# Attention scores of two heads together, in three passes over 64 rows each, in a one-core transformer block

## The chip, the cores and the metric

The kernel runs on one core of a Trainium2 chip. Its time is the device time of that core in microseconds, from three executions; a profiled execution of its own gives the trace. TensorE is called PE, its weight loads PEld, VectorE DVE, ScalarE ACT, GpSimd POOL and SyncE SP.

## The reference, cut to what matters

One residual block on a sequence of 1024 with model width 1024, in float32: a norm, one projection to the operands of eight stick-breaking heads and four differential heads of width 64 (each differential head has two score maps) and to two gates, the two attentions, output projections that are gated and added, a second projection, and a squared-ReLU MLP.

```python
z = jnp.einsum('bhqd,bhkd->bhqk', qb, kh).astype(jnp.float32) * scale      # stick-breaking
w = jnp.where(causal, jnp.exp(log_beta + tail), 0.0)
...
s = jnp.einsum('bhqd,bhkd->bhqk', qb, kh).astype(jnp.float32) * scale + bias   # differential
a = probs(q1b, k1h) - lam * probs(q2b, k2h)
```

A score sums over a head width of 64. TensorE is 128 rows high, and a matmul sums over its rows.

## The kernel before, in words

Matmuls run in a float32 form that rounds its operands, so the kernel splits each operand into a high part (the rounded value) and a low part (the rest) and adds products of parts. A projection takes three: high by high, high by low, low by high.

The attention is done in eight units, four of stick-breaking heads and four of differential ones; a unit holds two heads, or the two maps of one differential head. `project` computes 128 columns of the projection, which are the two heads' q (or k) one below the other: rows 0 to 63 and rows 64 to 127. `project_q` makes of this, for each head, one tile of 128 rows: the head's high part in its own 64 rows and its low part in the other 64. `project_k` makes, for each head, a tile with the high part and a tile with the low part, and copies each by DMA into the other 64 rows too. So a score needs two passes over all 128 rows: (q high over q low) with k high in both halves, and the same q with k low in both halves. `scores` issues these two matmuls (L262, L263) into one of two PSUM banks with the tag `sc`.

`steps_sb` goes through the two heads of a unit one after the other, each with the pairs of query tiles in the order 3, 1, 2, 0. For a query tile of 128 rows the keys up to the diagonal are taken in chunks of up to 512 columns. ScalarE empties a score bank with two sigmoids (L322, L323), GpSimd masks the diagonal block (L326), VectorE scans and multiplies (L331, L332). `steps_diff` does both maps of a query tile: VectorE adds the bias and keeps a running minimum (L389), ScalarE takes the exponential (L394). Score tiles come from pools: `big_s` of 1024 columns for query tiles 4 to 7 and `small_s` of 512 for the others, four buffers each.

When a pair of query tiles is done, `finish_sb` or `finish_diff` transposes the weights on PE (L281), splits them and multiplies them with v (L300, L301, or L342 to L344). These calls stand one step late, behind the next scores. Between the steps the main loop inserts filler: the projections of the next unit (L196 to L198, L243 to L245) and of the gates, dealt out in proportion to the steps' weights. What the program writes is then put in order by a scheduler, engine by engine, so matmuls written one after the other can end up with others between them; PE works strictly in that final order. A small matmul over 32 rows (L433, three times) builds the bias table between the first scores.

After the attention the outputs come back from DRAM as tiles `y` and go through the gated projections, the second projection and the MLP, which the change does not touch beyond the pools that `y` and the gates use.

Of the kernel before, what the change touches and what calls it, by code (L numbers as in the profile page):

```python
# [16 lines left out]
P = 128  # L17
# [24 lines left out]
def hybrid_block_kernel(  # L42
# [38 lines left out]
    def f32(ap):  # L81
        return ap.bitcast(F32)
# [67 lines left out]
    with ExitStack() as actx:  # L150
# [4 lines left out]
        def normalised(c):  # L155

            xs = []
            for t in range(4 * c, 4 * c + 4):
                if t == 6:
                    last = pa.tile([P, 2, D], F32, tag="v", name="x_67", bufs=3)  # L160
                if t < 6:
                    xt = pa.tile([P, D], F32, tag="big_s" if t < 4 else "kh", name=f"x_{t}", bufs=4)
                else:
                    xt = last[:, t - 6, :]
# [39 lines left out]
        def project_q(blk, name, scale, qs):  # L204

            qs += [pa.tile([P, S], F32R, tag="qs", name=f"qs_{name}_{a}", bufs=4) for a in range(2)]

            def done(c, cs, acc):
                for a, (own, other) in enumerate(((LO, HI), (HI, LO))):
                    nc.scalar.activation(qs[a][own, cs], acc[own], AF.Copy, scale=scale)  # L210
                    nc.vector.scalar_tensor_tensor(
                        qs[a][other, cs], acc[own], scale, f32(qs[a][own, cs]),
                        op0=ALU.mult, op1=ALU.subtract,
                    )

            yield from project(blk, name, done)

        def project_k(blk, name, kh, kl):

            kh += [pa.tile([P, S], F32R, tag="kh", name=f"kh_{name}_{a}", bufs=4) for a in range(2)]  # L220
            kl += [pa.tile([P, S], F32R, tag="kl", name=f"kl_{name}_{a}", bufs=4) for a in range(2)]

            def done(c, cs, acc):
                for a, own in enumerate((LO, HI)):
                    nc.scalar.copy(kh[a][own, cs], acc[own])
# [33 lines left out]
        def scores(qs, kh, kl, qt, c0, c1, name):  # L259
            z = ps.tile([P, HALF], F32, tag="sc", name=name, bufs=2)  # L260
            q = qs[:, qt * P:(qt + 1) * P]
            nc.tensor.matmul(z[:, :c1 - c0], q, kh[:, c0:c1], start=True, stop=False)  # L262
            nc.tensor.matmul(z[:, :c1 - c0], q, kl[:, c0:c1], start=False, stop=True)  # L263
# [48 lines left out]
        def steps_sb(u, qs, kh, kl, v):  # L312
            for a in range(2):
                for j in ORDER:
                    w = []
                    for qt in (2 * j, 2 * j + 1):
                        nk = (qt + 1) * P
                        name = f"{u}_{a}_{qt}"
                        beta, rest = score_tile(qt, f"beta_{name}"), score_tile(qt, f"rest_{name}")
                        for c0, c1 in chunks(nk):  # L320
                            z = scores(qs[a], kh[a], kl[a], qt, c0, c1, f"z_{name}_{c0}")
                            nc.scalar.activation(rest[:, c0:c1], z, AF.Sigmoid, scale=-1.0)  # L322
                            last_sigmoid[0] = nc.scalar.activation(beta[:, c0:c1], z, AF.Sigmoid)  # L323
                        dg = slice(nk - P, nk)
# [10 lines left out]
                        w.append(beta)  # L335
# [749 lines left out]
```

## Time and profile before

| | |
|---|---|
| median of 3 runs | 1466.37 us (1465.51 to 1468.13) |
| profiled execution | 1466.14 us, span 1464.4 us |
| granted TensorE clock | 0.999 |
| busy share of the span | PE 98%, PEld 83%, DVE 70%, ACT 51%, POOL 22% |
| matmuls | 7302 records |

A busy PE is not a PE at its peak, since matmuls overlap and their ends are modelled: the time from the start of one to the start of the next is what it occupies. In a timeline row the columns are the start, the length, the engine, the line, the operation, output and inputs, height and width of the weights, output shape and count, and in brackets the idle time before and what ended it. In a row of a group of instructions, the numbers behind the bar are busy time, mean length of one in ns, and idle time before them with what ended it.

### The profile page before, as it was taken

The numbers are of one execution on the slowest core, as the hardware profiler recorded it, in microseconds if no ns is written. First come the engines' busy times: TensorE is split into PE (matmuls) and PEld (weight loads), VectorE is DVE, ScalarE is ACT, GpSimd is POOL, SyncE is SP. The second block draws the span as 40 slices with busy tenths as digits, with TensorE's granted clock in tenths as the row PEclk, the third lists the DMA queues.
The fourth block names the chain that finished last, engine by engine and source line by source line (L and its number), as shares of the span: only waits on it lengthen the run. The fifth ranks groups of instructions, "written<-read, shape, count | busy, mean of one in ns | idle before, by whom it ended". The sixth has DMA issues, their size and how long they took to land. (4 is left out here: it accounts for less than half of the span.)

```text
span 1464.4 us, 20068 instructions
## 1 busy us (share of the span) xinstructions
PE 1437.3 (98%) x7302; PEld 1219.3 (83%) x7302; DVE 1021.1 (70%) x1468; ACT 743.2 (51%) x1352; POOL 322.4 (22%) x312
## 2 busy tenths in 40 slices
PE   7999999999999999999999989999999999999997
PEld 6888898899889888888888868788888778888886
DVE  5487987898779866535555489767664589764783
ACT  6356766676556645753434464444444344534450
POOL 2022231231000000000002326333330357232611
PEclk9999999999999999999999999999999999999999
DMA  5342212221322244554357735544445676677681
GB/s 205 77 133 66 69 48 80 68 70 51 91 72 67 85 136 173 178 181 146 131 159 233 244 115 195 182 158 147 139 155 200 216 274 190 200 239 273 203 287 58
DMA packets 93402, 219.45 MB, mean 150 GB/s; under 512 B 9228, under 2 KB 24824, under 8 KB 93304
## 3 DMA queue, kind: packets, MB, share of 16 engines
q1 hardware_dynamic: 78904, 198.25, 42.5%
q10 hardware_dynamic: 14400, 19.93, 3.7%
q8 instruction: 57, 0.93, 0.3%
q14 instruction: 41, 0.34, 0.1%
HBM read 152.07 MB, written 60.05 MB: 145 GB/s over the span
## 5 line engine op out<-in xcount | busy, mean ns | idle before, releaser
L331 DVE TENSOR_TENSOR_SCAN rest<-rest 128x896 f32<-128x896 f32 (+3 forms) x64 | 87.7, 1375 | 20.5 <-POOL rest L326 19.9
L198 PE MATMUL acc_gate<-h_hi,lo_gate 128*128 128x512 f32 x256 | 101.0, 394 | 0.0
L196 PE MATMUL acc_gate<-h_hi,hi_gate 128*128 128x512 f32 x256 | 100.8, 394 | 0.0
L197 PE MATMUL acc_gate<-h_lo,hi_gate 128*128 128x512 f32 x256 | 100.7, 393 | 0.0
L608 DVE TENSOR_TENSOR lS_lo<-raw_S,lS_hi 128x1024 fp32r<-128x1024 f32 x32 | 58.6, 1831 | 39.9 <-ACT lS_hi L607 39.8
L326 POOL TENSOR_SCALAR_AFFINE_SELECT rest<-rest 128x128 f32<-128x128 f32 x64 | 24.3, 379 | 239.7 <-ACT rest L322 223.2
L955 PE MATMUL dS<-rT_hi,lS_hi 128*128 128x512 f32 x192 | 74.7, 389 | 0.0
L955 PE MATMUL dS<-rT_lo,lS_hi 128*128 128x512 f32 x192 | 74.7, 389 | 0.0
L955 PE MATMUL dS<-rT_hi,lS_lo 128*128 128x512 f32 x192 | 74.7, 389 | 0.0
L607 ACT CAST lS_hi<-raw_S 128x1024 fp32r<-128x1024 f32 x32 | 33.7, 1052 | 78.2 <-DMA raw_S<-s_dramS 46.6
L567 PE MATMUL mix<-y,hi_mix 128*128 128x512 f32 x256 | 68.6, 389 | 0.0
L394 ACT ACTIVATE s<-s,low 128x896 f32<-128x896 f32 (+7 forms) x64 | 49.7, 776 | 28.0 <-DVE low L389 27.8
L389 DVE CUSTOM_DVE_ANT_0 s<-z,bias 128x512 f32<-128x512 f32 (+3 forms) x64 | 37.0, 587 | 31.7 <-PE z L263 26.7
L567 PEld LDWEIGHTS mix<-y,hi_mix 128*128 128x128 f32 x256 | 48.1, 188 | 9.9
L198 PEld LDWEIGHTS acc_gate<-h_hi,lo_gate 128*128 128x128 f32 x256 | 48.2, 188 | 9.2
L197 PEld LDWEIGHTS acc_gate<-h_lo,hi_gate 128*128 128x128 f32 x256 | 48.2, 188 | 8.8
L116 POOL TENSOR_SCALAR rstd_o<-s 128x1 f32<-128x1 f32 x8 | 3.0, 380 | 237.8 <-DMA grow<-in_g_rows_dram 213.0
L196 PEld LDWEIGHTS acc_gate<-h_hi,hi_gate 128*128 128x128 f32 x256 | 48.2, 188 | 8.6
L608 DVE TENSOR_TENSOR lA_lo<-raw_A,lA_hi 128x1024 fp32r<-128x1024 f32 x24 | 37.5, 1561 | 24.9 <-ACT lA_hi L607 23.3
L287 ACT CAST wth_sb<-tr_sb 128x512 fp32r<-128x512 f32 (+1 forms) x80 | 41.2, 548 | 26.5 <-PE tr_sb L281 25.1
L326 POOL TENSOR_SCALAR_AFFINE_SELECT beta<-beta 128x128 f32<-128x128 f32 x64 | 53.7, 838 | 3.2 <-ACT beta L323 2.1
L288 DVE TENSOR_TENSOR wtl_sb<-tr_sb,wth_sb 128x512 fp32r<-128x512 f32 (+1 forms) x80 | 48.5, 627 | 7.7 <-ACT wth_sb L287 7.5
(350 smaller groups left out, 4766.3 us busy)
## 6 DMA issues: line engine op xcount, KB each, us to landing
s_dramS<-us SPq DMA_DIRECT2D x64, 256.0 KB, 3.7
raw_S<-s_dramS SPq DMA_DIRECT2D x32, 512.0 KB, 4.6
s_dramA<-u ACTq DMA_DIRECT2D x48, 256.0 KB, 2.3
raw_A<-s_dramA SPq DMA_DIRECT2D x24, 512.0 KB, 3.9
raw_gate<-in_w_in_dram SPq DMA_DIRECT2D x16, 512.0 KB, 3.6
gate_dram<-gt SPq DMA_DIRECT2D x32, 256.0 KB, 2.4
y<-y_dram SPq DMA_DIRECT2D x16, 512.0 KB, 6.0
g<-gate_dram SPq DMA_DIRECT2D x16, 512.0 KB, 4.4
```

What stands on the lines that cost most here:

```text
L196: nc.tensor.matmul(acc, w_hi[:, ks], h_hi[k][:, cs], start=(k == 0), stop=False)
L197: nc.tensor.matmul(acc, w_hi[:, ks], h_lo[k][:, cs], start=False, stop=False)
L198: nc.tensor.matmul(acc, w_lo[:, ks], h_hi[k][:, cs], start=False, stop=(k == NK - 1))
L287: nc.scalar.copy(hi[:, :n], tr[:, :n])
L288: nc.vector.tensor_tensor(lo[:, :n], tr[:, :n], f32(hi[:, :n]), op=ALU.subtract)
L326: nc.gpsimd.affine_select(tl[:, dg], tl[:, dg], pattern=[[-1, P]], compare_op=ALU.is_gt, fill=fill, base=0, channel_multiplier=1,)
L331: nc.vector.tensor_tensor_scan(back, back, back, 1.0, op0=ALU.mult, op1=ALU.bypass)
L389: nc.vector.tensor_tensor_reduce(out=s[:, c0:c1], in0=z, in1=bias[:, S - nk + c0:S - nk + c1], scale=1.0, scalar=BIG if prev is None else ...
L394: e = nc.scalar.activation(s[:, :nk], s[:, :nk], AF.Exp, bias=low, scale=-1.0, accum_out=sums[:, m:m + 1],)
L567: nc.tensor.matmul(accs[i][c], st[:, ks], mv[:, cs], start=(first and k % 4 == 0), stop=(last and k % 4 == 3),)
L608: nc.vector.tensor_tensor(lo, raw, f32(hi), op=ALU.subtract)
L955: nc.tensor.matmul(acc, st[:, e, ts], mv[:, e, :], start=(first and e == 0 and i == 0), stop=(last and e == 1 and i == 2))
```

## The change

q and k are kept as projected: one tile of 128 rows with the high parts of both heads and one with the low parts, made by one function for both. The copies into the other half go. A score is now three passes over the 64 rows of its head (high q by high k, low q by high k, high q by low k), and the passes of the two heads are written alternately, rows 0 to 63 for the one and 64 to 127 for the other, each into its own `sc` bank. Both heads of a query tile are therefore worked on together, and their `finish` calls come together. Score tiles have six buffers of each kind; the tiles for `y`, the first x tiles and the first v weights move to other tags.

```diff
-        def project_q(blk, name, scale, qs):
-
-            qs += [pa.tile([P, S], F32R, tag="qs", name=f"qs_{name}_{a}", bufs=4) for a in range(2)]
+        def project_split(blk, name, tag, scale, parts):
+
+            parts += [pa.tile([P, S], F32R, tag=tag, name=f"{tag}_{name}_{p}", bufs=4) for p in range(2)]
+            hi, lo = parts
 
             def done(c, cs, acc):
-                for a, (own, other) in enumerate(((LO, HI), (HI, LO))):
-                    nc.scalar.activation(qs[a][own, cs], acc[own], AF.Copy, scale=scale)
-                    nc.vector.scalar_tensor_tensor(
-                        qs[a][other, cs], acc[own], scale, f32(qs[a][own, cs]),
-                        op0=ALU.mult, op1=ALU.subtract,
-                    )
+                nc.scalar.activation(hi[:, cs], acc, AF.Copy, scale=scale)
+                nc.vector.scalar_tensor_tensor(
+                    lo[:, cs], acc, scale, f32(hi[:, cs]), op0=ALU.mult, op1=ALU.subtract,
+                )
 
             yield from project(blk, name, done)
-
-        def project_k(blk, name, kh, kl):
...
-                for a, own in enumerate((LO, HI)):
-                    nc.scalar.copy(kh[a][own, cs], acc[own])
-                    nc.vector.tensor_tensor(kl[a][own, cs], acc[own], f32(kh[a][own, cs]), op=ALU.subtract)
-
-            yield from project(blk, name, done)
-            for a, (own, other) in enumerate(((LO, HI), (HI, LO))):
-                nc.sync.dma_start(out=f32(kh[a][other]), in_=f32(kh[a][own]))
-                nc.sync.dma_start(out=f32(kl[a][other]), in_=f32(kl[a][own]))
...
-        def scores(qs, kh, kl, qt, c0, c1, name):
-            z = ps.tile([P, HALF], F32, tag="sc", name=name, bufs=2)
-            q = qs[:, qt * P:(qt + 1) * P]
-            nc.tensor.matmul(z[:, :c1 - c0], q, kh[:, c0:c1], start=True, stop=False)
-            nc.tensor.matmul(z[:, :c1 - c0], q, kl[:, c0:c1], start=False, stop=True)
-            return z[:, :c1 - c0]
+        def scores(q, k, qt, c0, c1, name):
+
+            zs = [ps.tile([P, HALF], F32, tag="sc", name=f"{name}_{a}", bufs=2)[:, :c1 - c0] for a in range(2)]
+            for i, (qp, kp) in enumerate(((0, 0), (1, 0), (0, 1))):
+                for z, own in zip(zs, (LO, HI)):
+                    nc.tensor.matmul(
+                        z, q[qp][own, qt * P:(qt + 1) * P], k[kp][own, c0:c1], start=(i == 0), stop=(i == 2)
+                    )
+            return zs
 
         def score_tile(qt, name):
             if qt < 4:
-                return pa.tile([P, HALF], F32, tag="small_s", name=name, bufs=4)
-            return pa.tile([P, S], F32, tag="big_s", name=name, bufs=4)
+                return pa.tile([P, HALF], F32, tag="small_s", name=name, bufs=6)
+            return pa.tile([P, S], F32, tag="big_s", name=name, bufs=6)
...
-        def steps_sb(u, qs, kh, kl, v):
-            for a in range(2):
-                for j in ORDER:
-                    w = []
-                    for qt in (2 * j, 2 * j + 1):
...
+        def steps_sb(u, q, k, v):
+            for j in ORDER:
+                w = [[], []]
+                for qt in (2 * j, 2 * j + 1):
+                    nk = (qt + 1) * P
+                    tiles = [[score_tile(qt, f"{n}_{u}_{a}_{qt}") for n in ("beta", "rest")] for a in range(2)]
+                    for c0, c1 in chunks(nk):
+                        for (beta, rest), z in zip(tiles, scores(q, k, qt, c0, c1, f"z_{u}_{qt}_{c0}")):
                             nc.scalar.activation(rest[:, c0:c1], z, AF.Sigmoid, scale=-1.0)
                             last_sigmoid[0] = nc.scalar.activation(beta[:, c0:c1], z, AF.Sigmoid)
...
-                    yield 4 * j + 3, partial(finish_sb, u, a, j, w, v)
+                    yield 2 * qt + 2, [partial(finish_sb, u, a, j, w[a], v) for a in range(2)] if qt % 2 else []
```

`steps_diff` changes in the same way. What the scheduler makes of it is seen in PE's order. The rows name the line, the operation, output and inputs, and the output's shape. Before, a score bank is `z_head_querytile_firstcolumn_number`; the first unit's scores for query tile 4, head 0, are here, behind a projection of k:

```order
L198 MATMUL acc_sbk_0_965<-h_hi_162,lo_sbk_962 128x512
L262 MATMUL z_0_4_0_996<-kh_sbk_0_356,qs_sbq_0_325 128x512
L263 MATMUL z_0_4_0_996<-kl_sbk_0_358,qs_sbq_0_325 128x512
L262 MATMUL z_0_4_512_1001<-kh_sbk_0_356,qs_sbq_0_325 128x128
L263 MATMUL z_0_4_512_1001<-kl_sbk_0_358,qs_sbq_0_325 128x128
L300 MATMUL av_0_3_896<-wth_sb_0_3_0_902,v_sbv_0_389 128x256
```

Two matmuls make a bank, and head 1 follows nearly 200 rows later. With the change a bank is `z_querytile_firstcolumn_head_number`, and `q_sbq_0` and `k_sbk_0` are high parts, `_1` low parts. The same query tile in the first unit:

```order
L248 MATMUL z_4_0_0_1170<-k_sbk_0_354,q_sbq_0_325 128x512
L248 MATMUL z_4_0_0_1170<-k_sbk_0_354,q_sbq_1_326 128x512
L248 MATMUL z_4_0_0_1170<-k_sbk_1_355,q_sbq_0_325 128x512
L198 MATMUL acc_gate_1_1272<-h_hi_155,lo_gate_1135 128x512
L196 MATMUL acc_gate_1_1272<-h_hi_156,hi_gate_1134 128x512
L197 MATMUL acc_gate_1_1272<-h_lo_164,hi_gate_1134 128x512
L248 MATMUL z_4_0_1_1171<-k_sbk_0_354,q_sbq_0_325 128x512
L248 MATMUL z_4_0_1_1171<-k_sbk_0_354,q_sbq_1_326 128x512
L248 MATMUL z_4_0_1_1171<-k_sbk_1_355,q_sbq_0_325 128x512
```

The three passes of head 0 stand together, three matmuls of a gate's projection follow, and then the three passes of head 1: the alternation of the program text is gone here. At query tile 7 of the same unit it is kept:

```order
L198 MATMUL acc_sbq_1_829<-h_hi_162,lo_sbq_799 128x512
L248 MATMUL z_7_0_0_860<-k_sbk_0_354,q_sbq_0_325 128x512
L248 MATMUL z_7_0_1_861<-k_sbk_0_354,q_sbq_0_325 128x512
L248 MATMUL z_7_0_0_860<-k_sbk_0_354,q_sbq_1_326 128x512
L248 MATMUL z_7_0_1_861<-k_sbk_0_354,q_sbq_1_326 128x512
L248 MATMUL z_7_0_0_860<-k_sbk_1_355,q_sbq_0_325 128x512
L248 MATMUL z_7_0_1_861<-k_sbk_1_355,q_sbq_0_325 128x512
L196 MATMUL acc_sbk_0_904<-h_hi_155,hi_sbk_900 128x512
```

Heads 0 and 1 take turns, pass by pass. Over the whole program the 576 score matmuls stand in 158 groups with other matmuls between them; 132 pairs of neighbours in these groups are of different heads, and 312 score matmuls have no neighbour of the other head left to pair with.

More of the change, by code (lines that the diff above doesn't have):

```diff
@@ L475, in prepare @@
                 vs[u], vs[u + 1] = pair
[L476 removed]
+            operands[u] = (q, k, vs[u])
         n_units = N_SB + N_DIFF
@@ L506, in hybrid_block_kernel @@
                 pass
-        operands[0] = (qs, kh, kl, pair[0])
+        operands[0] = (q, k, pair[0])
         vs[1] = pair[1]
         setup_bias()
-        waiting = None
+        waiting = []
         for u in range(n_units):
@@ L519, in hybrid_block_kernel @@
             for weight, finish in (steps_sb(u, *operands[u]) if u < N_SB else steps_diff(u - N_SB, *operands[u])):
-                if waiting is not None:
-                    waiting()
+                for f in waiting:
+                    f()
                 waiting = finish
@@ L528, in hybrid_block_kernel @@
                 pass
-        waiting()
+        for f in waiting:
+            f()
         for b in range(GATES[-1].stop, 2 * NK):
```

66 lines of the change are left out of this document (28 added, 38 removed).

## The prediction

> **What bounds the kernel now.** First the windows view, which says in which stretch an engine has no room left, then the timeline of TensorE (PE) and of its weight loads (PEld) in that stretch, where the price of one matmul can be read from start to start. The columns of the windows are the stretch, then each engine's busy time and count, the granted clock, the DMA share and GB/s.
>
> ```profile
> PE 1437.3 (98%) x7302; PEld 1219.3 (83%) x7302; DVE 1021.1 (70%) x1468; ACT 743.2 (51%) x1352; POOL 322.4 (22%) x312
> 100.00:700.00 600.00, 598.62 (x3459) 525.80 (x3458) 451.47 (x895) 356.44 (x766) 67.35 (x116) 1.00 0.33 100
> L262 PE MATMUL z<-kh_sbk,qs_sbq 128*128 128x512 f32 (+2 forms) x96 | 34.7, 365 | 0.3 <-ACT beta L323 0.3
> L262 PE MATMUL z<-kh_dfk,qs_dfq 128*128 128x512 f32 (+3 forms) x96 | 33.8, 354 | 0.0
> L263 PE MATMUL z<-kl_sbk,qs_sbq 128*128 128x512 f32 (+2 forms) x96 | 32.7, 348 | 0.0
> L263 PE MATMUL z<-kl_dfk,qs_dfq 128*128 128x512 f32 (+3 forms) x96 | 32.6, 345 | 0.0
> ```
>
> In the 600 us that hold nearly all of the attention, PE is without a record for 1.4 us, at full clock. Time added to PE's stream there is added to the kernel; time taken from VectorE (451 of 600) or ScalarE (356 of 600) is hidden. The score matmuls are 4 x 96 = 384, and they waited 0.3 us in all. Their means (345 to 365 ns) are latencies that overlap, so I price them by starts:
>
> ```profile
> 79.40 0.39 PE L198 MATMUL acc_sbq<-h_hi,lo_sbq 128*128 128x512 f32 x1
> 79.63 0.33 PE L262 MATMUL z<-kh_sbk,qs_sbq 128*128 128x384 f32 x1
> 79.80 0.34 PE L263 MATMUL z<-kl_sbk,qs_sbq 128*128 128x384 f32 x1
> 79.97 0.40 PE L262 MATMUL z<-kh_sbk,qs_sbq 128*128 128x512 f32 x1
> 80.21 0.39 PE L263 MATMUL z<-kl_sbk,qs_sbq 128*128 128x512 f32 x1
> 80.44 0.82 PE L281 MATMUL tr_sb<-ident,beta 128*128 128x128 f32 x6
> ...
> 201.12 0.22 PE L262 MATMUL z<-kh_sbk,qs_sbq 128*128 128x128 f32 x1
> 201.18 0.28 PE L263 MATMUL z<-kl_sbk,qs_sbq 128*128 128x128 f32 x1
> 201.29 0.33 PE L262 MATMUL z<-kh_sbk,qs_sbq 128*128 128x256 f32 x1
> ...
> 307.57 0.28 PE L262 MATMUL z<-kh_sbk,qs_sbq 128*128 128x256 f32 x1
> 307.68 0.28 PE L263 MATMUL z<-kl_sbk,qs_sbq 128*128 128x256 f32 x1
> 307.80 0.28 PE L243 MATMUL acc_dfv<-hi_dfv,h_hi 128*128 128x256 f32 x1
> ```
>
> 512 columns take 0.23 us (79.40 to 79.63; 0.227 over a long row of them), 384 take 0.17 to 0.18, 256 take 0.12, and two of 128 take 0.17 together. Those last are held by the weight loads, one per matmul, which do not start closer than 0.11 us:
>
> ```profile
> 201.12 0.19 PEld L263 LDWEIGHTS z<-kl_sbk,qs_sbq 128*128 128x128 f32 x1
> 201.23 0.19 PEld L262 LDWEIGHTS z<-kh_sbk,qs_sbq 128*128 128x128 f32 x1
> 201.34 0.19 PEld L263 LDWEIGHTS z<-kl_sbk,qs_sbq 128*128 128x128 f32 x1
> ```
>
> **What the scores cost now.** A unit has two heads with eight query tiles each; by the key blocks up to the diagonal that is 6 chunks of 512 columns and two each of 384, 256 and 128, and 4 matmuls per chunk (2 passes, 2 heads): 24 x 0.227 + 8 x 0.175 + 8 x 0.12 + 8 x 0.085 = 8.49 us. Eight units: 67.9 us of PE.
>
> **Three passes instead of two.** 576 matmuls instead of 384. If each still takes its columns' time alone, the scores cost 1.5 x 67.9 = 101.9 us, +34.0. Only matmuls of the two heads that stand next to each other in PE's order can run in the two halves at once. Counted over the changed program's order, 132 such pairs stand there (57 of 512 columns, 21 of 384, 24 of 256, 29 of 128, one mixed); 288 would be all, and 312 passes have no partner. The trace of before has no two matmuls on different rows, so what a pair saves is bounded: nothing at one end, a whole matmul at the other (57 x 0.227 + 21 x 0.175 + 24 x 0.12 + 29 x 0.085 = 22.0 us). A pair still needs two loads, and by the PEld rows two loads take 0.22 us. I take that: a pair of 512 saves 0.227, one of 384 saves 0.35 - 0.22 = 0.13, one of 256 0.02, one of 128 nothing: 12.9 + 2.7 + 0.5 = 16.1 us. The scores then cost 85.8 us, **+17.9** (ends +12.0 and +34.0). The Trainium skill ("TensorE: Matmul & The Clock Gate", Part 3, packing small matmuls) says that matmuls on different row groups start about 4 ns apart, and gives 3.07x for four tiles of 32 rows; no row here shows it, and by it alone the pairs would save up to the 22 us.
>
> **Changing the tile's rows.** Each group of score matmuls now stands as a 64-row island among 128-row work. The changed order has 158 such groups. The only partial tile in the trace is the small matmul of 32 rows that builds the bias, between score matmuls:
>
> ```profile
> 64.05 0.28 PE L245 MATMUL acc_sbv<-qs_sbv,h_lo 128*128 128x256 f32 x1
> 64.26 0.80 PE L433 MATMUL bp<-oh,tbl 32*4 32x384 f32 x2
> 65.00 0.50 PE L262 MATMUL z<-kh_sbk,qs_sbq 128*128 128x512 f32 x1
> 65.33 0.40 PE L263 MATMUL z<-kl_sbk,qs_sbq 128*128 128x512 f32 x1
> 65.57 0.33 PE L262 MATMUL z<-kh_sbk,qs_sbq 128*128 128x384 f32 x1
> 65.74 0.34 PE L263 MATMUL z<-kl_sbk,qs_sbq 128*128 128x384 f32 x1
> 66.01 1.45 PE L433 MATMUL bp<-oh,tbl 32*4 32x384 f32 x4
> ...
> 64.26 0.09 PEld L433 LDWEIGHTS bp<-oh,tbl 32*4 32x4 f32 x2
> 64.99 0.19 PEld L262 LDWEIGHTS z<-kh_sbk,qs_sbq 128*128 128x128 f32 x1 [0.65 <-ACT v_sbv L254]
> 65.10 0.19 PEld L263 LDWEIGHTS z<-kl_sbk,qs_sbq 128*128 128x128 f32 x1
> ```
>
> Going in, the matmul of 256 columns should end its slot at 64.05 + 0.12 = 64.17, and the 32-row one starts at 64.26: 0.09 late. The second time the slot ends at 65.74 + 0.175 = 65.92 and the start is 66.01: 0.09 again. Coming out, the two 32-row records of 0.32 each end at 64.90 and the score matmul starts at 65.00: 0.10 late. Its load started at 64.99, not one matmul ahead as everywhere else, so the next matmul comes after 0.33 instead of 0.23: 0.10 more. Equal delays at three places speak for the change of shape and against a chance wait. In and out together: 0.09 + 0.10 + 0.10 = 0.29 us. Nor does a mere change of operation explain it, for around full-height transposes nothing is lost: six of them at 0.109 and one matmul of 0.227 make 0.88, which is 306.45 to 307.33:
>
> ```profile
> 306.45 0.81 PE L281 MATMUL tr_sb<-ident,beta 128*128 128x128 f32 x6
> 307.02 0.48 PE L262 MATMUL z<-kh_sbk,qs_sbq 128*128 128x512 f32 x1
> 307.33 0.39 PE L263 MATMUL z<-kl_sbk,qs_sbq 128*128 128x512 f32 x1
> ```
>
> 158 x 0.29 = **+45.8 us**. Below: 0, if 64 rows of full width are no change of shape to PE. Above: 0.39 a group, since going in now also has a full load of 128 columns to expose (the 32-row tile had 4): 61.6 us. The Trainium skill ("TensorEngine Tiling (Array Packing)", Key Properties) says that changing the tiling mode drains TensorE; the 0.09 and 0.10 us agree. By that rule alone, without a price, this term is above nothing; without the rule it could be left out, and the sum would be 1484.
>
> **What is removed.** The unit's q and k are split with one copy and one subtraction per half sequence instead of two, and the four copies between partition halves go:
>
> ```profile
> L211 DVE SCALAR_TENSOR_TENSOR qs_sbq<-acc_sbq,qs_sbq x16: 683/688/694, 31.7 to 229.6; 64x512 fp32r<-64x512 f32 x16
> L225 ACT CAST kh_sbk<-acc_sbk x16: 570/582/593, 31.5 to 242.7; 64x512 fp32r<-64x512 f32 x16
> kh_sbk<-kh_sbk SPq DMA_DIRECT2D x8, 256.0 KB, 3.0
> ```
>
> 32 operations less on VectorE (22 us at 0.69) and on ScalarE (19 us at 0.58), 32 transfers less on SP's queue. All of it runs beside a PE that idles 1.4 us in 600, so I price it at **0**; the most it could give is those 1.4 us. If PE were not the bound it would be worth up to 22 us.
>
> **Score tiles and PSUM.** Two heads need eight big score tiles per pair of query tiles where one head needed four; six are there, so two wait for the scan of the tile before. The score banks stay two, and both heads take one each, so the second pass of an alternating group cannot start before ScalarE has emptied both (two sigmoids of 0.55 us each per bank, by the row below). Behind that wait stand PE's transposes and projections. PE is slower than before while the others have less to do, so I take 0 here, and keep up to 35 us for the range: 32 groups alternate fully, at 1.1 us each.
>
> ```profile
> L322 ACT ACTIVATE rest<-z x96: 264/549/617, 66.6 to 344.3; 128x512 f32<-128x512 f32 x48, 128x384 f32<-128x384 f32 x16, 128x128 f32<-128x128 f32 x16, 128x256 f32<-128x256 f32 x16
> L323 ACT ACTIVATE beta<-z x96: 261/546/630, 67.1 to 344.6; 128x512 f32<-128x512 f32 x48, 128x384 f32<-128x384 f32 x16, 128x128 f32<-128x128 f32 x16, 128x256 f32<-128x256 f32 x16
> ```
>
> **The sum.** The profiled execution took 1466.1 us, of which the span is 1464.4, and the median of the three runs is 1466.4, so nothing is to be corrected between them: 1466.1 + 17.9 + 45.8 = **1530**.
>
> **Rivals.**
> Going between 64 and 128 rows is free. For it: the 32-row tile was also narrow (4 columns), so its delay may come from the columns. Against it: the delay is there in both directions. 1466.1 + 17.9 = 1484, or 1478 where loads overlap too. Chance 0.20.
>
> The halves do not run at once, and the change doesn't do what it says even where the order alternates. The trace can say nothing against it. 1466.1 + 34.0 + 45.8 = 1546. Chance 0.13.
>
> The wait for both score banks takes PE's time. For it: the longest group of waits that a score matmul had was for ScalarE (0.3 us). Against it: it is only 0.3 us. Half of 35 us on top of the forecast: 1548. Chance 0.10.
>
> Faster: a 64-row pass, with or without a partner, takes half of its columns' time, so three cost 1.5 full ones instead of 2. The place is every score matmul, the price 0.75 x 67.9 = 50.9, so -17.0 and 1449; it decides as soon as a pass costs less than two thirds of a full one and the shape change is free. Against it: the 32-row record takes 0.32 us for 384 columns ((1.45 - 0.48) / 3), no less than full rows do. Chance 0.05.
>
> **How the numbers follow.** The forecast has 0.52, its own range 1512 (half of the shape price, 0.145 a group) to 1548 (0.39 a group and a little waiting). The range runs from 1478, the free shape change, to 1562, where the halves do not overlap and the shape change costs 0.39: 1466.1 + 34.0 + 61.6. What a measurement of this kernel can tell from no change is 0.2%, 3 us. Faster has the 0.05 of the last rival; a sum within 3 us would need the shape change free and 15 us from elsewhere, 0.02; slower is 0.93.
>
> **What would show it.** In the changed profile: two score matmuls of different heads that start within some 10 ns of each other in an alternating group (overlap right) or 0.23 us apart (wrong); a gap of about 0.1 us and a load without lead at both ends of a score group (shape price right) or none; 576 score matmuls; the attention ending some 64 us later, and all after it as before. Wrong would be a time below 1478, or a PE that idles more than a few us in the attention.

## The result, and the profile after

With the change the kernel takes **1541.79 us** (median of four executions, 1537.57 to 1545.12) against 1466.36 us before: 75 us more, a ratio of 1.0511 with a 95% interval of 1.0482 to 1.0541. The profiled execution took 1540.35 us, its span 1538.5 us at a mean clock of 0.996. The forecast was 1530 in a range of 1478 to 1562. So the side and the mechanism were right, and the time lies 10 to 12 us above the forecast.

First the page of the changed kernel: busy time, share of the span and count of each engine, then the two score groups (busy time, mean of one in ns, idle time before them and what ended it).

```profile
PE 1508.3 (98%) x7494; PEld 1226.3 (80%) x7494; DVE 998.4 (65%) x1436; ACT 725.1 (47%) x1320; POOL 328.9 (21%) x312
L248 PE MATMUL zd<-k_dfk,q_dfq 64*128 64x512 f32 (+3 forms) x288 | 62.0, 381 | 0.2 <-DVE low L373 0.2
L248 PE MATMUL z<-k_sbk,q_sbq 64*128 64x512 f32 (+3 forms) x288 | 58.9, 381 | 0.4 <-ACT beta L308 0.4
```

There are 7494 matmuls instead of 7302, the 576 score matmuls instead of 384. They waited 0.6 us in all, so the two score banks are no new wait. The other engines lost work as planned (DVE 998.4 us instead of 1021.1, ACT 725.1 instead of 743.2), and it bought nothing.

Where the time went is seen from the first operation behind the attention, the gated projections `mix`. The view of one tile's instructions gives shortest, median and longest duration in ns, then the first and the last start in us. Before:

```profile
L567 PE MATMUL mix<-y,lo_mix x128: 389/389/389, 655.0 to 740.9; 128*128 128x512 f32 x128
```

and after:

```profile
L552 PE MATMUL mix<-y,lo_mix x128: 389/389/389, 728.1 to 814.0; 128*128 128x512 f32 x128
```

They begin 73.1 us later and take 85.9 us in both. So 73.1 of the 74.1 us by which the span grew lie ahead of them, and nearly nothing behind.

Now the stretch of that time, by engine as in the prediction (stretch, busy time and count of PE, PEld, DVE, ACT and POOL, granted clock, DMA share, GB/s). Of the changed kernel, with 60 us more since the attention ends later:

```profile
100.00:760.00 660.00, 655.76 (x3612) 524.88 (x3611) 431.00 (x865) 340.19 (x745) 73.11 (x119) 0.99 0.24 77
```

PE is without a record for 4.2 us instead of 1.4, and still far busier than the others: 2.9 us are new waits, the other 70 are inside PE's stream.

**Inside the stream.** The timeline of TensorE in the changed kernel, at an alternating group of six passes and at a group of three (start, length, engine, line, operation, tiles, shapes, count):

```profile
80.01 0.39 PE L198 MATMUL acc_sbq<-h_hi,lo_sbq 128*128 128x512 f32 x1
80.33 0.97 PE L248 MATMUL z<-k_sbk,q_sbq 64*128 64x512 f32 x6
81.23 0.50 PE L196 MATMUL acc_sbk<-h_hi,hi_sbk 128*128 128x512 f32 x1
81.57 0.40 PE L197 MATMUL acc_sbk<-h_lo,hi_sbk 128*128 128x512 f32 x1
...
86.57 0.39 PE L198 MATMUL acc_sbk<-h_hi,lo_sbk 128*128 128x512 f32 x1
86.89 0.96 PE L248 MATMUL z<-k_sbk,q_sbq 64*128 64x512 f32 x3
87.78 0.49 PE L196 MATMUL acc_sbk<-h_hi,hi_sbk 128*128 128x512 f32 x1
```

Six passes take from 80.33 to 81.23, 0.90 us; three alone take from 86.89 to 87.78, 0.89. **The second head is free where it stands beside the first.** Three columns' times are 3 x 0.227 = 0.68, so 0.22 of each group is not matmul, and there is more on both sides: the group starts 0.32 behind a matmul that occupies 0.227 (0.09 late), and the matmul behind the group holds PE for 0.34 instead of 0.227 (0.11 late). That makes 0.09 + 0.22 + 0.11 = 0.42 us here. Taken over the records of all 158 groups the medians are 0.093 going in, 0.105 behind the first pass (its load had no lead), 0.096 coming out and 0.107 behind the first full matmul: **0.40 us a group**.

The loads show the missing lead (the bracket is the idle time before). In the first row a load runs one matmul ahead (the matmul of L198 starts at 80.01); then the group's loads start with the group, and so does the first load behind it:

```profile
79.79 0.19 PEld L198 LDWEIGHTS acc_sbq<-h_hi,lo_sbq 128*128 128x128 f32 x1
80.33 0.53 PEld L248 LDWEIGHTS z<-k_sbk,q_sbq 64*128 64x128 f32 x6 [0.35 <-issue]
81.23 0.19 PEld L196 LDWEIGHTS acc_sbk<-h_hi,hi_sbk 128*128 128x128 f32 x1 [0.37 <-issue]
```

How the pairs run is seen in narrow windows over the score matmuls of the group of six alone (busy time and count of PE, then of PEld):

```profile
80.32:80.35 0.03, 0.02 (x2) 0.02 (x2) 1.00 0.66 273
80.35:80.64 0.29, 0.29 (x2) 0.28 (x4) 1.00 0.49 198
80.64:80.68 0.04, 0.04 (x4) 0.01 (x2) 1.00 0.25 102
```

Two matmuls and two loads are begun within the first 30 ns. For the next 0.29 us no third matmul begins, while the loads of the next pair come in. Then four are counted: two that end and the two that begin. In the records the two of a pair start 1 to 14 ns apart, most of them 3 to 10. So the two loads of a pair run at the same time too, and do not follow each other by 0.11 us as the full-height loads of the scores do. Pairs of 384 columns start every 0.17 to 0.18 us and pairs of 128 every 0.11, both less than the 0.22 of two loads in a row.

**The waits and the clock.** The longest wait in the attention (start, length, operation; in the bracket the wait and what ended it):

```profile
338.36 0.36 PE L227 MATMUL acc_dfv<-hi_dfv,h_hi 128*128 128x256 f32 x1 [2.05 <-DVE v_dfv L239]
```

VectorE's own timeline there:

```profile
335.70 0.94 DVE L317 TENSOR_TENSOR_SCAN rest<-rest 128x384 f32<-128x384 f32 x1
337.01 1.02 DVE L317 TENSOR_TENSOR_SCAN rest<-rest 128x384 f32<-128x384 f32 x1 [0.37 <-POOL rest L312]
337.95 0.46 DVE L239 TENSOR_TENSOR v_dfv<-acc_dfv,v_dfv 128x128 fp32r<-128x128 f32 x2
```

PE's next projection of v waits for VectorE's split of the last one (L239). That stands behind the scans of both heads, the second of which itself waits for GpSimd's mask. VectorE, idle a third of the time, is late at this one place. And behind the stall the clock drops, as a window shows:

```profile
340.00:342.00 2.00, 2.00 (x9) 1.68 (x8) 2.00 (x5) 0.08 (x1) 0.80 (x2) 0.50 0.00 0
```

PE runs at 0.50 for 6.8 us (339.9 to 346.7), which costs 3.4 us more. So this stall of 2.05 us cost 5.4 in all. Not every stall does that: the next longest of this attention, 1.66 us at 692 us, left the clock alone.

### The profile page after: what moved, and what is told of

Read it like the earlier page. It is cut to its first block, busy times and chain, and to the rows that moved or that the text cites. A ratio compares the mean times of both kernels' runs of the same rounds, so it can differ in the third digit from the quotient of the medians.

```text
span 1538.5 us, 20230 instructions
## 1 busy us (share of the span) xinstructions
PE 1508.3 (98%) x7494; PEld 1226.3 (80%) x7494; DVE 998.4 (65%) x1436; ACT 725.1 (47%) x1320; POOL 328.9 (21%) x312
## 5 line engine op out<-in xcount | busy, mean ns | idle before, releaser
L198 PE MATMUL acc_gate<-h_hi,lo_gate 128*128 128x512 f32 x256 | 102.4, 400 | 0.0
L317 DVE TENSOR_TENSOR_SCAN rest<-rest 128x896 f32<-128x896 f32 (+7 forms) x64 | 87.6, 1375 | 15.9 <-POOL rest L312 15.5
L312 POOL TENSOR_SCALAR_AFFINE_SELECT rest<-rest 128x128 f32<-128x128 f32 x64 | 34.6, 541 | 275.0 <-ACT rest L307 275.0
L307 ACT ACTIVATE rest<-z 128x512 f32<-128x512 f32 (+3 forms) x96 | 47.2, 492 | 31.8 <-PE z L248 27.0
L248 PE MATMUL zd<-k_dfk,q_dfq 64*128 64x512 f32 (+3 forms) x288 | 62.0, 381 | 0.2 <-DVE low L373 0.2
L248 PE MATMUL z<-k_sbk,q_sbq 64*128 64x512 f32 (+3 forms) x288 | 58.9, 381 | 0.4 <-ACT beta L308 0.4
L198 PEld LDWEIGHTS acc_gate<-h_hi,lo_gate 128*128 128x128 f32 x256 | 48.1, 188 | 13.1 <-issue 3.8
```

Source lines behind the costliest of these rows:

```text
L198: nc.tensor.matmul(acc, w_lo[:, ks], h_hi[k][:, cs], start=False, stop=(k == NK - 1))
L248: nc.tensor.matmul(z, q[qp][own, qt * P:(qt + 1) * P], k[kp][own, c0:c1], start=(i == 0), stop=(i == 2))
L317: nc.vector.tensor_tensor_scan(back, back, back, 1.0, op0=ALU.mult, op1=ALU.bypass)
```

## The experiments

Each timed run has four executions, beside seven of the kernel before on the same chip (medians 1466.4 to 1467.1).

### The loops over two heads alone: all 128 rows

```diff
-                        z, q[qp][own, qt * P:(qt + 1) * P], k[kp][own, c0:c1], start=(i == 0), stop=(i == 2)
+                        z, q[qp][:, qt * P:(qt + 1) * P], k[kp][:, c0:c1], start=(i == 0), stop=(i == 2)
```

> The changed kernel with the same order of instructions on PE, but every score pass takes all 128 rows, so that it sums over both heads (the scores are therefore not those of the reference). No change of shape and no overlap are left; the loops over two heads, the three passes and the six score tiles stay. Theory (three passes cost 1.5 times two, +34 us; the shape change costs about 0.39 us for each of 158 groups, 62 us; overlap saves 22 to 27 us): 1466 + 34 = 1500 us, and up to 5 more for waits. Rival (the shape change is free, the loss comes from the order and its waits): only the overlap is lost, 1542 + 25 = 1567 us.

Measured: 1513.6 us (1510.61 to 1519.26), ratio 1.0332 (1.0297 to 1.0367). PE's order is that of the changed kernel to the row; only the height differs. The same place in the timeline:

```profile
80.40 0.39 PE L198 MATMUL acc_sbq<-h_hi,lo_sbq 128*128 128x512 f32 x1
80.63 1.52 PE L248 MATMUL z<-k_sbk,q_sbq 128*128 128x512 f32 x6
81.99 0.39 PE L196 MATMUL acc_sbk<-h_hi,hi_sbk 128*128 128x512 f32 x1
82.22 0.39 PE L197 MATMUL acc_sbk<-h_lo,hi_sbk 128*128 128x512 f32 x1
```

Six full passes take 1.36 = 6 x 0.227, the start is 0.23 behind the last matmul and the next comes 0.23 later: no delay at either end. So what stands at the ends of a 64-row group comes with the height, not with a new accumulation, another bank or another kind of operand. The time is above what three passes make (half of the 69.5 us that two passes take, with 0.11 for 128 columns, is 34.8, so 1501), and above the 1505 that were expected at most. The longest waits of the attention are most of the rest (engine and what it was to do, what ended the wait, total in us, times, longest):

```profile
PE tr_df L268 <- DVE s L388: 2.7, 1, 2.7
PE acc_dfv L227 <- DVE v_dfv L239: 2.6, 1, 2.6
```

and the window:

```profile
100.00:760.00 660.00, 651.28 (x3745) 571.14 (x3744) 447.50 (x892) 350.11 (x758) 71.42 (x119) 1.00 0.26 84
```

PE is without a record for 8.7 us instead of 1.4, which is 7.3 us more. Another 1.7 come from 3.4 us at half clock, but these lie behind the attention (892 us), after a stall of 2.05 us there. 1466.1 + 34.8 + 7.3 + 1.7 = 1509.9; the profiled execution took 1510.61. Working on two heads at once has a price of its own, about 7 us here, that the forecast had at 0.

Behind the longest stall of the attention, 2.72 us that end at 662.00, the clock does not fall:

```profile
662.00:670.00 8.00, 8.00 (x39) 6.79 (x40) 3.73 (x7) 6.33 (x12) 0.00 (x0) 1.00 0.88 332
```

### No overlap: both heads in rows 0 to 63

```diff
-                for z, own in zip(zs, (LO, HI)):
+                for z, own in zip(zs, (LO, LO)):
```

> The changed kernel with the same order on PE, but the passes of both heads take rows 0 to 63 (the second head's scores are those of the first). The shape changes stay, the overlap goes. Theory (the halves overlap): 1542 + 22 to 27 = 1564 to 1569 us. Rival (the records only look as if they overlapped, each pass takes its columns' time): 1542 us, no change.

Measured: 1565.8 us (1563.35 to 1571.86), ratio 1.0681 (1.065 to 1.0713), 24 us above the changed kernel. Order and shapes are the same, so the 24 us are what the second half is worth, net of waits and clock. Those differ a little: the changed kernel's profiled execution holds 6.3 us of new waits and half clock, this one 1.7. With that the second half is worth some 28 us, where counting passes gives 26.7. The group of six:

```profile
80.72 1.66 PE L248 MATMUL z<-k_sbk,q_sbq 64*128 64x512 f32 x6
82.31 0.50 PE L196 MATMUL acc_sbk<-h_hi,hi_sbk 128*128 128x512 f32 x1
```

1.59 us instead of 0.90; the difference is three matmuls of 0.227. The overlap is real, and it is at least 24 us and not the 16.1 of the forecast, which let the loads limit a pair and counted fewer pairs.

### A change of height away from the scores: one gate matmul of three over 64 rows, then over 32

In the kernel before, the middle matmul of each gate step sums over rows 0 to 63 alone, 256 times, with everything else in place:

```diff
+            rows = slice(0, 64 if blk >= GATE else P)
-                    nc.tensor.matmul(acc, w_hi[:, ks], h_lo[k][:, cs], start=False, stop=False)
+                    nc.tensor.matmul(acc, w_hi[rows, ks], h_lo[k][rows, cs], start=False, stop=False)
```

> The kernel before, its order unchanged; only the middle pass of the three in the projections of the 16 gates (high weights by low activations) takes rows 0 to 63 instead of all 128, so half of this small correction is left out of the gates. The columns, the number of matmuls and everything else stay: 256 single 64-row matmuls between full ones, in a place that has nothing to do with scores. Theory (a price for each group of 64 rows, 0.09 + 0.10 us on the way in and the same out): 1466 + 256 x 0.39 = 1566 us. At the price that the prediction took, 0.29: 1541 us. Rival (the shape change is free): 1466 us.

Measured: 1571.26 us (1569.55 to 1573.2), ratio 1.0708 (1.0689 to 1.0727). That is 104.1 us for 256 islands, **0.407 us each**, with no score touched. The timeline:

```profile
109.23 0.39 PE L197 MATMUL acc_gate<-h_hi,hi_gate 128*128 128x512 f32 x1
109.56 0.50 PE L198 MATMUL acc_gate<-h_lo,hi_gate 64*128 64x512 f32 x1
109.98 0.50 PE L199 MATMUL acc_gate<-h_hi,lo_gate 128*128 128x512 f32 x1
110.32 0.39 PE L197 MATMUL acc_gate<-h_hi,hi_gate 128*128 128x512 f32 x1
```

Three matmuls take 1.09 us instead of 0.68, in the same four parts: 0.33 - 0.227 going in, 0.42 - 0.227 for the exposed load and coming out, 0.34 - 0.227 for the next exposed load.

With 32 rows in place of 64 (`rows = slice(0, 32 if blk >= GATE else P)`):

> The kernel before, order unchanged, with the middle pass of the gates' projections over rows 0 to 31 (three quarters of this small correction left out): 256 single matmuls of 32 rows between full ones. Theory (the price is that of a change of shape, whatever the rows): as with 64 rows, 1571 us within 5. Rival (the price grows as the rows shrink): clearly more.

Measured: 1571.6 us (1569.59 to 1572.66), ratio 1.0701 (1.0663 to 1.0739), 0.411 us each. The price is the same for 32 rows and for 64. The bias matmul that the forecast took its 0.29 from had 32 rows as well; what it lacked was a full load, since its weights have 4 columns. With a load of 128 columns the same 32 rows cost 0.41.

### Per change or per matmul: two of three, and all three

The third gate matmul over 64 rows as well:

```diff
-                    nc.tensor.matmul(acc, w_lo[:, ks], h_hi[k][:, cs], start=False, stop=(k == NK - 1))
+                    nc.tensor.matmul(acc, w_lo[rows, ks], h_hi[k][rows, cs], start=False, stop=(k == NK - 1))
```

> The kernel before, with the second and the third pass of the gates' projections over rows 0 to 63 (half of both corrections is left out): 512 matmuls of 64 rows in 290 groups. Theory (the price is per group): 1466 + 290 x 0.39 = 1579 us. Rival (the price is per 64-row matmul): 1466 + 512 x 0.39 = 1666 us.

Measured: 1602.92 us (1589.99 to 1605.81, three executions), ratio 1.0897 (1.0844 to 1.095); a fourth, of 1620.45 us at a clock of 0.972, is not in these figures. The three lie 16 us apart, and their mean clocks are 0.992, 0.986 and 0.983. The profiled one is the shortest. A window of it:

```profile
116.00:123.00 7.00, 7.00 (x21) 4.79 (x20) 0.62 (x2) 2.51 (x6) 0.29 (x1) 0.52 0.01 2
```

Here PE never waits and the clock is 0.52. This happens three times in that attention (17 us), while PE's gaps are 1.3 us in 660. Without the 8.5 to 10.2 us that it costs, the profiled execution is 114 to 115 us above the kernel before; its order has 290 groups, so 0.39 to 0.40 each. The price fits "per group", but a run whose clock moves by itself proves little, so the next has the opposite: many low matmuls, few changes.

All three over 64 rows, which makes 768 matmuls in 89 groups:

```diff
-                    nc.tensor.matmul(acc, w_hi[:, ks], h_hi[k][:, cs], start=(k == 0), stop=False)
+                    nc.tensor.matmul(acc, w_hi[rows, ks], h_hi[k][rows, cs], start=(k == 0), stop=False)
```

> The kernel before with all three passes of the gates' projections over rows 0 to 63 (half of each sum is left out): 768 matmuls of 64 rows in only 89 groups. Theory A (only the change of shape costs): 1466 + 89 x 0.39 = 1501 us, clock as before. Theory B (dense 64-row work alone also lowers the granted clock, as the runs with two 64-row passes in a row, clock 0.972 to 0.992 with hardly any idling, suggest): clearly above 1501 us, with stretches of half clock in the gates where TensorE is not idle.

Measured: 1504.19 us (1502.08 to 1511.37), ratio 1.0253 (1.0213 to 1.0293). 37.8 us for 89 groups are 0.42 each, in the shortest execution 0.40; for 768 matmuls it would be 0.05 each, which the timeline does not show:

```profile
109.18 0.49 PE L197 MATMUL acc_gate<-h_hi,hi_gate 64*128 64x512 f32 x1
109.51 0.39 PE L198 MATMUL acc_gate<-h_lo,hi_gate 64*128 64x512 f32 x1
109.75 0.39 PE L199 MATMUL acc_gate<-h_hi,lo_gate 64*128 64x512 f32 x1
```

The attention in one window:

```profile
100.00:760.00 660.00, 658.67 (x3574) 541.29 (x3574) 469.73 (x919) 367.53 (x785) 68.25 (x119) 1.00 0.31 96
```

Behind the first, 64-row matmuls follow each other every 0.23 us like full ones, and the clock stays at 1.00. So the price is paid **once for each group, whatever is in it**. It also settles that a 64-row pass alone costs its columns' time and not half of it. Nor do low matmuls lower the clock when they come in long rows, as in this execution (0.999).

### Fewer groups: one tile of two banks for both heads

Since a group costs 0.40 and a group of six no more than one of three, the six passes of a chunk should stay together. In the changed kernel the scheduler splits them, because the two heads' banks come free at different times. One tile that spans both banks comes free at once:

```diff
-            zs = [ps.tile([P, HALF], F32, tag="sc", name=f"{name}_{a}", bufs=2)[:, :c1 - c0] for a in range(2)]
+            both = banks[0].tile([P, 2, HALF], F32, tag="sc", name=name, bufs=1)
+            zs = [both[:, a, :c1 - c0] for a in range(2)]
```

> The changed kernel with one PSUM tile of two banks for the two heads' scores instead of two tiles of one bank, so that the six passes of a chunk become ready together and stand together: 106 groups instead of 158, nearly all alternating. Nothing is left out. Theory: passes 53.3 us instead of 69.5 (loads no limit to a pair), -16; 106 x 0.39 = 41; so 1466 + 25 = 1491 us, up to 8 more because a chunk now waits until both banks are empty. Rival (waits for score banks are what costs): slower than 1542 us.

Measured: 1515.01 us (1512.18 to 1519.98), ratio 1.0332 (1.0305 to 1.036). It is 27 us better than the changed kernel and still 48.5 slower than before. There are 106 groups instead of 158, and all passes are paired: 53.3 us of passes instead of 69.5. The sum by these alone, 1466.1 - 16.2 + 106 x 0.40, is 1492. The time is 16 us above the 1499 that were expected at most. What came on top, first the longest waits and then the window:

```profile
PE tr_sb L279 <- DVE beta L329: 5.0, 2, 2.5
PE acc_sbv L237 <- DVE v_sbv L249: 2.4, 2, 2.1
```

```profile
100.00:760.00 660.00, 646.18 (x3730) 529.29 (x3729) 447.22 (x892) 348.39 (x757) 75.48 (x122) 0.99 0.26 82
```

PE is without a record for 13.8 us instead of 1.4 (12.4 more), and 17 us run at half clock (8.5 lost). 1492.3 + 12.4 + 8.5 = 1513.2, and the profiled execution took 1514.81. When both heads' scores are done together, the transposes and the projections of v find VectorE still busy with scans.

### The order inside a group

As before, but the three passes of one head are written first and those of the other behind them:

```diff
-            for i, (qp, kp) in enumerate(((0, 0), (1, 0), (0, 1))):
-                for z, own in zip(zs, (LO, HI)):
+            for z, own in zip(zs, (LO, HI)):
+                for i, (qp, kp) in enumerate(((0, 0), (1, 0), (0, 1))):
```

PE's final order has them so (a `-` row is the kernel with the two-bank tile, a `+` row this one; x2 is one pass of each head):

```
-L259 MATMUL z_6_0_765<-k_sbk_0_357,q_sbq_0_328 128x512 x2
-L259 MATMUL z_6_0_765<-k_sbk_0_357,q_sbq_1_329 128x512 x2
-L259 MATMUL z_6_0_765<-k_sbk_1_358,q_sbq_0_328 128x512 x2
+L259 MATMUL z_6_0_765<-k_sbk_0_357,q_sbq_0_328 128x512
+L259 MATMUL z_6_0_765<-k_sbk_0_357,q_sbq_1_329 128x512
+L259 MATMUL z_6_0_765<-k_sbk_1_358,q_sbq_0_328 128x512
+L259 MATMUL z_6_0_765<-k_sbk_0_357,q_sbq_0_328 128x512
+L259 MATMUL z_6_0_765<-k_sbk_0_357,q_sbq_1_329 128x512
+L259 MATMUL z_6_0_765<-k_sbk_1_358,q_sbq_0_328 128x512
```

> The kernel with the two-bank tile, but the three passes of the first head are written ahead of the three of the second: 106 groups again, 86 of them with three passes of one half and then three of the other. Theory A (PE starts a pass as soon as its half is free, also ahead of earlier ones of the other half, as groups of this form in the changed kernel's trace suggest, with starts 10, 325, 10, 225 and 10 ns apart): within 3 us of the kernel with the two-bank tile, 1494 us. Theory B (PE starts passes strictly in order, so one pair in five slots): 87 us of passes instead of 53, 1525 us.

Measured: 1515.94 us (1512.96 to 1519.9), ratio 1.0337 (1.031 to 1.0364): the same as with alternating passes. If PE kept the written order, only the last pass of one head could meet the first of the other, and it would be some 30 us slower. The timeline of TensorE:

```profile
87.08 0.39 PE L206 MATMUL acc_sbk<-h_hi,hi_sbk 128*128 128x512 f32 x1
87.39 0.97 PE L259 MATMUL z<-k_sbk,q_sbq 64*128 64x512 f32 x6
88.30 0.50 PE L207 MATMUL acc_sbk<-h_lo,hi_sbk 128*128 128x512 f32 x1
```

0.91 us for six, as in the alternating group. Over the whole trace 270 pairs of score matmuls start together, against 282 with alternating passes. And the narrow windows over this group's score matmuls:

```profile
87.38:87.42 0.04, 0.03 (x2) 0.03 (x2) 1.00 0.00 0
87.42:87.70 0.28, 0.28 (x2) 0.28 (x4) 1.00 0.00 0
87.70:87.74 0.04, 0.04 (x4) 0.01 (x1) 1.00 0.00 0
```

Two matmuls are begun at once and two more 0.3 us later: the fourth in order starts with the first. So the halves each keep their own order, and matmuls of one half overtake those of the other that wait. What is said ahead of the prediction, that PE works strictly in its final order, holds within a half only. The Trainium skill ("TensorE: Matmul & The Clock Gate", Part 3, the mechanism) says that matmuls of packed tiles start and end strictly in program order. This run differs from it, and the measurement decides; the same part's 4 ns between the starts of packed matmuls lies in the 3 to 10 ns of most pairs here.

### Still fewer groups: four banks at a time

If six passes in a group gain little, twelve in one could gain more: two chunks of both heads in a tile of four banks. PSUM has to give the banks, one each from the transposes and from the weighted sums:

```diff
-            both = banks[0].tile([P, 2, HALF], F32, tag="sc", name=name, bufs=1)
-            zs = [both[:, a, :c1 - c0] for a in range(2)]
+            four = banks[0].tile([P, 4, HALF], F32, tag="sc", name=name, bufs=1)
+            zs = [[four[:, 2 * n + a, :c1 - c0] for a in range(2)] for n, (qt, c0, c1) in enumerate(items)]
```

> The kernel with a score tile of four PSUM banks: both chunks of a query tile above 512 keys, or both query tiles of a smaller pair, are scored together, in 65 groups. To make room, the transposes and the weighted sums have one bank each during the attention instead of two. Nothing is left out. Theory: passes 53.6 us instead of 69.5, -16; 65 x 0.39 = 25; 1466 + 9 = 1476 us, plus what the missing banks cost in waits (bound: 20 us). Rival (grouping brings no more, waits grow with it): slower than the two-bank tile.

Measured: 1611.73 us (1608.08 to 1613.76), ratio 1.0977 (1.0958 to 1.0996), with 65 groups, which alone would give 1466.1 - 16.2 + 26 = 1476. The longest wait (total in us, times, longest) and the attention in one window:

```profile
PE av L308 <- DVE part L312: 31.0, 14, 5.2
```

```profile
100.00:760.00 660.00, 590.51 (x3296) 485.94 (x3296) 397.15 (x807) 300.46 (x684) 68.73 (x116) 0.89 0.20 63
```

With one bank for the weighted sums, PE waits until the last one is emptied. It stands for 69.5 us instead of 1.4, and the clock is 0.89 (150 us at half clock), which over 660 us costs 73. 1476 + 68 + 73 = 1617, within 6 of the time. The loss by the lower clock is as large as the waits.

The groups of this trace tell the price apart from the waits. One of twelve passes begins at 79.06 us, 0.31 behind the matmul before it; its six slots of 512 columns last until 80.65, and the matmul behind it holds PE for 0.34. By the same parts as above that is 0.09 + 0.23 + 0.11 = 0.43 us, so twelve passes pay what three pay.

Two banks for the weighted sums again, and one for the projections:

```diff
-        return banks[0].tile([P, HALF], F32, tag=tag, name=name, bufs=banks[1])
+        return banks[0].tile([P, HALF], F32, tag=tag, name=name, bufs=2 if tag == "av" else banks[1])
```

> The kernel with a score tile of four PSUM banks again, in 56 groups, but now the weighted sums keep their two banks and the projections' accumulator has one instead: with one bank for the weighted sums TensorE stood for 69 us in the attention and its clock fell to half for 75 us around that. Nothing is left out. Theory (passes 52.7 us instead of 69.5; 56 x 0.39 = 22): 1466 + 5 = 1471 us with no waits; with waits W on TensorE the time is 1471 + W plus half of the time at half clock, both read from its trace. Rival (the price falls less than the groups): more than 10 us above that sum.

Measured: 1647.05 us (1644.78 to 1653.76), ratio 1.1225 (1.1183 to 1.1266), with 56 groups. Longest waits, and a window that holds the attention:

```profile
PE av L308 <- DVE wtl_sb L295: 25.3, 29, 4.1
PE av L307 <- ACT wth_sb L294: 18.1, 26, 1.3
PE acc_gate L205 <- ACT gt L464: 12.4, 10, 3.0
```

```profile
90.00:770.00 680.00, 579.93 (x3318) 475.28 (x3319) 412.79 (x838) 321.89 (x717) 72.24 (x123) 0.93 0.20 62
```

The weighted sums still wait, now for the split and the copy of the weights whose transposes have one bank, and the projections wait for theirs. 1466.1 - 16.2 + 22.4 + 98.7 of waits + 47.6 by the clock = 1619, and the profiled execution took 1645.19, 26 us more. Most of these lie outside the window: over the whole span PE is without a record for 138.9 us against 27.2 before (111.7 more), and 106 us ahead of its end run at half clock (52.9 lost). With these the sum is 1637, and 8 us stay open. So the time gives no ground for a price that falls less than the groups, and no sharp figure for it either; in neither of the two layouts tried with eight banks does grouping further pay.

## Why the prediction was right, and where its sizes were off

The account of the changed kernel and of the runs that bear on it, each against its profiled execution. Base is 1466.1; waits are PE's time without a record in the stretch from 100 to 760 us beyond the 1.4 of before; the clock is half of the time at half clock (with 128 rows it lies behind the attention). The sums end between 3.4 above the time and 1.6 below it:

| kernel | passes | groups x 0.40 | waits | clock | sum | measured |
|---|---|---|---|---|---|---|
| the change | +8.1 | 158: 63.2 | 2.9 | 3.4 | 1543.7 | 1540.35 |
| 128 rows | +34.8 | 0 | 7.3 | 1.7 | 1509.9 | 1510.61 |
| both heads in one half | +34.8 | 158: 63.2 | 1.7 | 0 | 1565.8 | 1563.64 |
| two-bank tile | -16.2 | 106: 42.4 | 12.4 | 8.5 | 1513.2 | 1514.81 |

- **What bounds the kernel** was right. 73.1 of 74.1 us lie in the attention, inside PE's stream or in PE's waits.
- **Three passes, +34.0**: right. With full height and the same order it is 34.8 by the sum that fits to 1 us.
- **What a pair saves, 16.1 us**: too small. The step that failed is "two loads take 0.22 us. I take that". The loads of the two halves run at once, and a pair costs what one matmul costs. The count failed too: 132 pairs were counted as neighbours in the final order, but PE pairs within a whole group whatever the order in it, and 149 pairs start together in the trace. By the longer half of each group the passes cost 77.6 us, so +8.1 against 69.5 before (or +9.7 against the forecast's own 67.9), below its lower end of +12.0. The run in one half measures the gain as 24 us, or some 28 without the difference in waits and clock.
- **The change of shape, 0.29 a group**: the mechanism was right, the size was not. It is 0.40, just above the end of 0.39 that was kept for the exposed load going in, and this is why: the load of the first 64-row pass costs 0.105 more. 158 groups are 63.2 us instead of 45.8. It was shown apart from the scores (0.407 and 0.411) and by its absence (128 rows: none).
- **Score banks, 0 (up to 35)**: right, 0.6 us.
- **Removed work, 0**: right. ScalarE and VectorE got 18 and 23 us shorter, and the time did not.
- **Not in the sum**: two heads at once put the scans of both in a row on VectorE, so PE's next projection of v or transposes come late (2.9 us), and the clock fell behind one such stall (3.4 us). The forecast weighed a wait for the score banks and not for what else stands in VectorE's queue.

The errors of the first two sizes are +17.4 (shape) and -9.8 (passes). They cancel in part, and with 6.3 of waits and clock they make 13.9 over 1530; the measured times are 10 (profiled) and 12 (median) over it. That the forecast came so near is luck to that extent: with the shape alone put right it would have been 1547. The lower end of its own range, 1512, does not follow from its terms either: 17.9 and 158 x 0.145 give 1507.

The time alone does not choose among the rivals: 1541.79 is nearer to 1546 (no overlap) and 1548 (waits for the banks) than to 1530. The runs choose: the free change of shape fell (0.41 us at each of 256 places with nothing else changed). The halves that do not run at once fell (24 us). The wait for both banks fell (0.6 us). The half-price pass fell: 64-row matmuls follow each other every 0.23 us. What was to be seen in the profile was seen: starts within some 10 ns, 0.1 us and a load without lead at both ends, 576 matmuls, nothing new behind the attention. Only its end came 73 us later and not 64.

Could it win at all? A fully paired chunk of 512 columns needs three slots of 0.227 instead of four for two heads: 0.23 us gained, against 0.40 for the group. At 106 groups the passes gain 16.2 us, while groups (42.4), waits (12.4) and clock (8.5) cost 63.3, so 47 of these would have to go. Of the layouts tried, four banks only moved the price into waits.

## What to carry to other kernels

Packing two half-height matmuls is worth what it seems (a pair takes the time of one), but each stay at the other height costs about 0.40 us here, whether it holds one matmul (0.41) or a dozen (0.43). Count the stays in the final order, not the matmuls, and compare the gain of one stay with that price. When a change doubles what comes in a row on a neighbouring engine, look for what else stands in that engine's queue, and look at the clock behind a stall of PE of some 2 us: one of 2.05 us cost 5.4, one of 2.72 only itself.

## What the runs showed of the hardware that was not expected

- **The halves go out of the written order.** Three passes of one half and then three of the other run as three pairs in 0.91 us, as six alternating passes do in 0.90.
- **The loads of the two halves overlap.** Pairs of 128 columns, with two loads each, follow every 0.11 us, which is the distance of single full-height loads of the scores.
- **The price of a change of height** has four parts of about 0.1 us: two in starting late at either end, and two loads without their lead. 32 and 64 rows cost the same.
- **A short stall can halve the clock.** After 2.05 us without work PE ran at 0.50 for 6.8 us. The Trainium skill ("TensorE: Matmul & The Clock Gate", Part 1) has the clock fall after an idle window of about 3.4 us. The 6.8 us are two such windows, but a stall of 2.05 us was enough, which the page does not have. The length alone does not decide: with 128 rows, stalls of 2.62 and 2.72 us left the clock at 1.00. In all traces of this case the stretches at half clock, save those at a kernel's very end, last whole multiples of 3.41 us (3.4, 6.8, 10.2 and so on to 34.1) and begin whole multiples of 3.41 apart within a trace. So where a stall falls in that raster may decide; this was not tested.
- **The clock can fall with no stall at all**: 17 us at half clock where two of three gate matmuls were half height and the height changed every half microsecond or so, with a PE that never waited. One of three (256 islands) or all three (89 groups) left the shortest executions at 0.999. Why the mixture does it is open.
